# Merge stage of a transformer block: one written order on four engines, and two kinds of weight and activation splits on VectorE

## The chip, the cores and the metric

The kernel runs on one core of a Trainium2 chip. Its engines take instructions from queues of their own: PE (TensorE, matrix products), DVE (VectorE), ACT (ScalarE), POOL (GpSimd) and SP (SyncE, which here only issues DMA transfers). The metric is the device time of one execution in microseconds (us). It is the median over several runs.

## The reference

One layer over 2048 latent tokens of width 1024 with a context of 256 tokens. What matters here is the last part of the token-mixing half: two branch results are projected to the model width, gated, added, and projected once more onto the residual.

```python
def branch_merge(attn_o, gm_o, ga_logit, gb_logit, w_br_attn, w_br_gm, w_out):
    y = jax.nn.sigmoid(ga_logit) * (attn_o @ w_br_attn) + jax.nn.sigmoid(gb_logit) * (gm_o @ w_br_gm)
    return y @ w_out
...
        x = x + g1 * branch_merge(attn_x, gm_x, ga_x, gb_x, w_br_attn[l], w_br_gm[l], w_out[l])

        h2 = modulate(x, norm2_g[l], sh2, sc2)
        x = x + g2 * sq_relu_mlp(h2, w_ff1[l], w_ff2[l])
```

`attn_o` and `gm_o` are 2048 x 512, `w_br_attn` and `w_br_gm` 512 x 1024, `w_out` 1024 x 1024. Everything is float32.

## The kernel before

A float32 product is made of three products of rounded operands. Each operand is split in a high part (a cast on ACT, line 144 in `split`) and a low part (the operand less its high part, line 148, on POOL or DVE as the argument `lo_eng` says); `mm3` (lines 176 to 178) then multiplies high by high, high by low and low by high. Line 177 needs the low part of the moving operand, line 178 that of the stationary one.

The merge (`merge`) comes after attention and before the feed-forward half. It works through four blocks of 512 tokens (`NB`), each in two stages.

- **Branch stage.** Eight steps m (`KC`), one for each 128 output channels. A step has 24 matmuls: 12 for the gMLP branch "g" and 12 for the attention branch "a", into two of the eight PSUM banks. Then DVE multiplies each bank by its gate (line 910, twice), adds the two (line 913), and the sum y(m) is split: high on ACT, low on POOL.
- **Output product.** Four token tiles of 128 (tt), two halves n of 512 columns each: 192 matmuls of y with the split `wo` of `w_out`. The first tile runs k = 0 to 6 for both halves before k = 7, so that y(7) is needed last. After each half DVE scales (line 954) and adds to the residual tile `xt` (line 955); the tile is stored (line 957) and ACT sums its squares (line 960).

Three flows feed this. `fetch` is called at the start of step m and brings the branch weights (`br_raw`, line 859, tile `bw`, 14 slots), splits them (`br_weights`) and brings the gates (`gate_in`, line 874, tile `gt`, 6 slots) for the step two ahead, also over the border between blocks: at steps 6 and 7 it fetches for steps 0 and 1 of the next block, at step 0 for step 2. While the output product of block b runs, the generator `br_inputs(b + 1)`, moved on after each half, loads the next block's branch inputs (line 838; for attention also the softmax scales, line 842, multiplied in by DVE on line 848) and splits them into tile `in`. The slots of `raw` (3), `xt` (3) and `bw` make a load wait until whatever read the slot before is done. Block 0's branch stage also loads and splits `w_out` (line 826, tiles `ws` and `wo`).

The order of the instructions on an engine is set by a scheduler that weighs costs and slots; a written order holds only where `order()` adds a dependence. That function runs at the very end over all instructions: those in `pinned` ranges, and on PE and DVE those in `fixed` ranges, on SP those in `loads` ranges, are made to follow the one written before them on their engine. No such range lies in the merge's blocks, so there the scheduler chooses:

```python
            held = idx in pinned or (idx in fixed and i.engine in engines)
            held = held or (idx in loads and i.engine == self.nc.sync.engine)
            after = keys + ([i.engine] if held else [])
            for prev in {last[k].name for k in after if k in last}:
                self.tc.add_manual_dep(i, prev, dep, reason="order")
```

In this merge 20 of the 64 low splits of branch weights are on DVE (block 0's fetches and the first two), the other 44 and all 32 low splits of y on POOL. Low splits of `in` and `wo` are on DVE.

Of the kernel before, what the change touches and what calls it, by code (L numbers as in the profile page):

```python
# [67 lines left out]
class Kern:  # L68
    def __init__(self, ctx, tc, I, out):
        self.tc, self.nc, self.I, self.out = tc, tc.nc, I, out  # L70
        self.ctx = ctx
        self.uid = 0
        self.tags = {}
        self.pins = []
        self.fixed = []
        self.loads = []
        self.open_pools, self.pool_of = {}, {}
        self.banks = None
# [780 lines left out]
            self.nc.sync.dma_start(out[nm], src.rearrange("(k p) c -> p k c", p=P))  # L859
        return out  # L860

    def br_weights(self, raw, lo_eng="pool"):
        ws = {}
        for nm in ("g", "a"):
            wh, wl = self.sb("bw", [4, P], F32R), self.sb("bw", [4, P], F32R)
            self.split(raw[nm], wh, wl, lo_eng=lo_eng)
            ws[nm] = (wh, wl)
        return ws

# [8 lines left out]
    def merge(self, first, start, last):  # L878
        nc = self.nc
        for _ in start:  # L880
            pass
        self.close("mid", "base")
        self.open("out")
        self.open("branch")
        steps = [(b, m) for b in range(NB) for m in range(KC)]
        it = iter(steps)
        q = []
        w_out = self.load_w_out()

        def fetch(lo_eng="pool"):  # L890
            s = next(it, None)
            if s is not None:
                q.append((self.br_weights(self.br_raw(s[1]), lo_eng), self.gate_in(*s)))

        inp = first
        early = [(s, self.br_raw(s[1])) for s in (next(it), next(it))]
        for s, raw in early:
            q.append((self.br_weights(raw, "dve"), self.gate_in(*s)))
        for b in range(NB):
            y = []  # L900
            for m in range(KC):
                fetch("pool" if b else "dve")
                ws, gt = q.pop(0)
                for nm in ("g", "a"):
                    ps = self.bank([TB])
                    wh, wl = ws[nm]
                    for k in range(4):
                        h, l = inp[nm][k]
                        self.mm3(ps, wh[:, k, :], wl[:, k, :], h, l, k == 0, k == 3)
                    nc.vector.scalar_tensor_tensor(  # L910
                        out=gt[nm], in0=gt[nm], scalar=1.0, in1=ps, op0=ALU.add, op1=ALU.mult
                    )
                nc.vector.tensor_tensor(out=gt["a"], in0=gt["a"], in1=gt["g"], op=ALU.add)
                yh, yl = self.sb("y", [TB], F32R), self.sb("y", [TB], F32R)
                self.split(gt["a"], yh, yl)
                y.append((yh, yl))
                if b == 0:
                    next(w_out, None)
                    if m == 2:
                        last.sums(self.sb("raw", [TB]))  # L920
                    if m == 4:
                        last.inverse()
            inp = {}
            if b + 1 < NB:
                side = self.br_inputs(b + 1, inp)
            else:
                self.close("branch", "pre")
                self.open("early", side="right")
                side = self.h_early()
                next(side)  # L930
            for tt in range(TT):
                tok = slice(tt * P, (tt + 1) * P)
                xt = self.sb("xt", [D])
                nc.sync.dma_start(xt, self.x_block(b)[tok, :])
                banks = [self.bank([512]) for _ in range(2)]

                def outer(n, ks):
                    cs = slice(n * 512, (n + 1) * 512)
                    for k in ks:
                        self.mm3(  # L940
                            banks[n], y[k][0][:, tok], y[k][1][:, tok], self.wo[k][0][:, cs],
                            self.wo[k][1][:, cs], k == 0, k == KC - 1,
                        )

                head = KC - 1 if tt == 0 else KC
                if tt == 0:
                    for n in range(2):
                        outer(n, range(head))
                for n in range(2):
                    cs = slice(n * 512, (n + 1) * 512)  # L950
                    ps = banks[n]
                    outer(n, range(head if tt == 0 else 0, KC))
                    part = self.sb("jk", [512])
                    nc.vector.tensor_tensor(out=part, in0=ps, in1=self.g1b[:, cs], op=ALU.mult)
                    nc.vector.tensor_tensor(out=xt[:, cs], in0=xt[:, cs], in1=part, op=ALU.add)
                    next(side, None)
                nc.sync.dma_start(self.x1_d[b][tok, :], xt)
                junk = self.sb("jk", [D], mybir.dt.bfloat16)
                col = b * TT + tt
                nc.scalar.activation(  # L960
                    junk, xt, AF.Square, accum_out=self.ss2[:, col : col + 1]
                )
            for _ in side:
                pass
# [477 lines left out]
    def order(self):  # L1442
        dep = mybir.DependencyInfo(mybir.DependencyClass.NoSync, mybir.DependencyReason.DATA)
        last, seen = {}, set()
        pinned = {n for r in self.pins for n in r}
        fixed = {n for r in self.fixed for n in r}
        loads = {n for r in self.loads for n in r}
        engines = (self.nc.tensor.engine, self.nc.vector.engine)
        for idx, i in enumerate(list(self.nc.cur_bb.bb.instructions)):
            keys = []  # L1450
            for o in i.outs:
                n = getattr(getattr(o, "bass_ap", None), "name", None)
                if n in self.tags and n not in seen:
                    seen.add(n)
                    keys.append(self.tags[n])
            held = idx in pinned or (idx in fixed and i.engine in engines)
            held = held or (idx in loads and i.engine == self.nc.sync.engine)
            after = keys + ([i.engine] if held else [])
            for prev in {last[k].name for k in after if k in last}:
                self.tc.add_manual_dep(i, prev, dep, reason="order")  # L1460
            for k in keys + [i.engine]:
                last[k] = i
# [242 lines left out]
```

## Time and profile before

| | |
|---|---|
| median of 3 runs | 3104.24 us (3098.3 to 3105.01) |
| the profiled execution | 3103.83 us, of which the profile's span is 3102.0 us (1.83 us lie around it) |
| mean granted clock of TensorE | 0.994 |
| busy: PE, DVE, ACT, POOL | 3042.7, 1972.1, 1356.6, 704.1 us |
| matmuls | 13892 |
| the merge's blocks (branch stage of block 0 to the start of the feed-forward half) | 1456.2 to 1830.5 us from the span's start |

The profile is of one execution. A row of a group reads: line, engine, operation, out<-in with buffer numbers left out, shapes, count, then the sum of busy time and the mean ns of one, then the idle time of the engine just before them and what ended it. L148 and L144 are lines of the helper `split`, so the tile tells which use is meant: `bw`, `y`, `in` or `wo`. In the table by stage, each engine has its busy us and instruction count, and the last three numbers are the granted TensorE clock, the busy share of the DMA engines and GB/s. POOL, DVE and ACT work on 128 x 512 tiles here, and PE's matmul of a step is 128 x 128 by 128 x 512.

### The profile page before, as it was taken

The numbers are of one execution on the slowest core, as the hardware profiler recorded it, in microseconds if no ns is written. First come the engines' busy times: TensorE is split into PE (matmuls) and PEld (weight loads), VectorE is DVE, ScalarE is ACT, GpSimd is POOL, SyncE is SP. The second block draws the span as 40 slices with busy tenths as digits, with TensorE's granted clock in tenths as the row PEclk, the third lists the DMA queues.
The fourth block names the chain that finished last, engine by engine and source line by source line (L and its number), as shares of the span: only waits on it lengthen the run. The fifth ranks groups of instructions, "written<-read, shape, count | busy, mean of one in ns | idle before, by whom it ended". The sixth has DMA issues, their size and how long they took to land.

```text
span 3102.0 us, 37971 instructions
## 1 busy us (share of the span) xinstructions
PE 3042.7 (98%) x13892; PEld 2299.5 (74%) x13892; DVE 1972.1 (64%) x2893; ACT 1356.6 (44%) x2058; POOL 704.1 (23%) x539
## 2 busy tenths in 40 slices
PE   8999999999999999999999999999999999999999
PEld 4888888887555555555877878887777888888777
DVE  5837576576776767667643488876654676654545
ACT  4443435342555554544322255444543344444433
POOL 0000000010888888886144300000000000000000
PEclk9999999999999999999999999999999999999999
DMA  6354756544000000003754548887575644445565
GB/s 218 111 175 120 226 156 192 165 142 132 26 14 15 15 4 18 11 8 118 253 180 156 164 148 320 315 306 256 201 246 210 210 150 155 157 147 192 204 216 204
DMA packets 332173, 485.42 MB, mean 156 GB/s; under 512 B 33969, under 2 KB 166321, under 8 KB 331986
## 3 DMA queue, kind: packets, MB, share of 16 engines
q1 hardware_dynamic: 324002, 478.38, 46.3%
q10 hardware_dynamic: 7984, 4.61, 0.5%
q8 instruction: 109, 1.79, 0.2%
q14 instruction: 78, 0.64, 0.1%
HBM read 348.56 MB, written 134.35 MB: 156 GB/s over the span
## 4 chain that ended last, share of the span: by engine, by line
PE 89%; DMA 5%; DVE 3%; ACT 1%; issue 1%; POOL 1%; SPq 0%; DVEq 0%; ACTq 0%; POOLq 0%
PE b L1196 12%; PE b L1197 12%; PE b L1195 11%; PE b L176 10%; PE b L178 10%; PE b L177 10%; PE b L1597 8%; PE b L1564 5%; PE b L1583 4%; PE b L1529 3%; PE b L182 2%; DMA f<-w2o_d 1%; DMA bw<-in_w_br_gm 1%; POOL bw L148 1%; DMA f<-x_d 1%
## 5 line engine op out<-in xcount | busy, mean ns | idle before, releaser
L1292 DVE TENSOR_TENSOR f<-f,f 128x1024 fp32r<-128x1024 f32 x224 | 273.2, 1224 | 274.6 <-ACT f L1291 271.0
L1540 DVE TENSOR_REDUCE ts<-b 128x1 f32<-128x512 f32 x512 | 314.6, 681 | 173.2 <-PE b L1529 173.2
L1291 ACT CAST f<-f 128x1024 fp32r<-128x1024 f32 x224 | 235.2, 1053 | 335.3 <-DMA f<-ao_d 288.9
L1196 PE MATMUL b<-f,f 128*128 128x512 f32 x896 | 351.3, 392 | 4.6 <-DVE f L1292 4.0
L1197 PE MATMUL b<-f,f 128*128 128x512 f32 x896 | 349.6, 390 | 0.0
L1195 PE MATMUL b<-f,f 128*128 128x512 f32 x896 | 307.4, 392 | 10.3 <-ACT b L1334 4.7
L1613 POOL TENSOR_TENSOR ac<-ac,p 128x512 f32<-128x512 f32 x216 | 296.6, 1406 | 71.1 <-ACT p L1587 70.4
L1587 ACT ACTIVATE p<-b 128x512 f32<-128x512 f32 x384 | 199.4, 615 | 159.3 <-PE b L1583 142.5
L1613 POOL TENSOR_TENSOR ac<-ac,t 128x512 f32<-128x512 f32 x160 | 231.9, 1476 | 1.4 <-ACT t L1587 1.4
L1196 PE MATMUL b<-hl,f 128*128 128x512 f32 x576 | 224.9, 391 | 1.6 <-DVE hl L971 1.5
L1195 PE MATMUL b<-hl,f 128*128 128x512 f32 x576 | 224.1, 389 | 0.0
L1197 PE MATMUL b<-hl,f 128*128 128x512 f32 x576 | 224.0, 389 | 0.0
L148 DVE TENSOR_TENSOR w<-w,w 128x1024 fp32r<-128x1024 f32 x120 | 146.6, 1222 | 99.1 <-ACT w L144 70.6
L1195 PEld LDWEIGHTS b<-f,f 128*128 128x128 f32 x896 | 168.1, 188 | 51.0 <-ACT f L1291 6.8
L176 PE MATMUL b<-t,w 128*128 128x512 f32 x512 | 202.8, 396 | 0.1
L1196 PEld LDWEIGHTS b<-f,f 128*128 128x128 f32 x896 | 168.8, 188 | 45.7 <-DVE f L1292 11.2
L1564 PE MATMUL b<-t,t 128*128 128x512 f32 x576 | 198.4, 415 | 1.7 <-ACT p L1587 1.6
L178 PE MATMUL b<-t,w 128*128 128x512 f32 x512 | 199.7, 390 | 0.0
L177 PE MATMUL b<-t,w 128*128 128x512 f32 x512 | 199.5, 390 | 0.0
L1197 PEld LDWEIGHTS b<-f,f 128*128 128x128 f32 x896 | 168.5, 188 | 34.6
L176 PE MATMUL b<-w,t 128*128 128x512 f32 (+1 forms) x528 | 191.0, 362 | 1.0 <-ACT t L440 1.0
L144 ACT CAST w<-w 128x1024 fp32r<-128x1024 f32 x120 | 126.1, 1050 | 150.0 <-DMA w<-in_w_in 118.3
(226 smaller groups left out, 6289.6 us busy)
## 6 DMA issues: line engine op xcount, KB each, us to landing
w<-in_w_in SPq DMA_DIRECT2D x120, 512.0 KB
ao_d<-f SPq DMA_DIRECT2D x224, 256.0 KB
f<-ao_d SPq DMA_DIRECT2D x112, 512.0 KB
f<-w2o_d SPq DMA_DIRECT2D x112, 512.0 KB
f<-in_w_ff SPq DMA_DIRECT2D x48, 1024.0 KB
w2o_d<-f SPq DMA_DIRECT2D x112, 256.0 KB
md<-in_w_mod SPq DMA_DIRECT2D x32, 512.0 KB
f<-x_d SPq DMA_DIRECT2D x64, 256.0 KB
```

Of the source, the lines that this page charges most:

```text
L176: mm(ps, sh, mh, start=start, stop=False)
L177: mm(ps, sh, ml, start=False, stop=False)
L178: mm(ps, sl, mh, start=False, stop=stop)
L1195: mm(ps, wh, hh, start=start and k == 0, stop=False, skip_group_check=True)
L1196: mm(ps, wh, hl, start=False, stop=False, skip_group_check=True)
L1197: mm(ps, wl, hh, start=False, stop=k == len(w) - 1, skip_group_check=True)
L1291: nc.scalar.copy(h, f32(l))
L1292: nc.vector.tensor_tensor(out=l, in0=f32(l), in1=f32(h), op=ALU.subtract)
L1540: nc.vector.tensor_reduce(out=self.mx[:, t, h, c : c + 1], in_=ps[h], axis=AX.X, op=ALU.max)
L1564: self.nc.tensor.matmul(self.pts[j][h], k.KA[c][self.kv][:, ks], self.qa[h], start=True, stop=False, skip_group_check=True,)
L1597: nc.tensor.matmul(self.o[h * HD : (h + 1) * HD, :], k.V[c][:, i, self.kv * HD : (self.kv + 1) * HD], pt[h], start=j == 0, stop=j == NKT - 1,)
L1613: nc.gpsimd.tensor_tensor(out=self.acc[e][:, h], in0=old[:, h], in1=pt[h], op=ALU.add)
```

## The change

Every low split of the branch weights and of y is now made on DVE; POOL has nothing left in the merge (it loses 76 instructions, DVE gains 76). And a new range, from the end of block 0's branch stage to the end of block 3's branch stage, is held in written order on every engine but SP. SP stays with the scheduler, whose choice there comes out differently as well. On PE the order of all instructions is the same as before.

```diff
         self.fixed = []
+        self.steady = []
...
-    def br_weights(self, raw, lo_eng="pool"):
+    def br_weights(self, raw):
...
-            self.split(raw[nm], wh, wl, lo_eng=lo_eng)
+            self.split(raw[nm], wh, wl, lo_eng="dve")
...
-                self.split(gt["a"], yh, yl)
+                self.split(gt["a"], yh, yl, lo_eng="dve")
...
             inp = {}
+            if b == 0:
+                begin = self.here()
             if b + 1 < NB:
                 side = self.br_inputs(b + 1, inp)
             else:
+                self.steady.append(range(begin, self.here()))
                 self.close("branch", "pre")
...
+        steady = {n for r in self.steady for n in r}
...
             held = idx in pinned or (idx in fixed and i.engine in engines)
+            held = held or (idx in steady and i.engine != self.nc.sync.engine)
             held = held or (idx in loads and i.engine == self.nc.sync.engine)
```

The lines of the changed file lie one to six further down (L144 is L145, L148 is L149, L859 is L860, L874 is L875, L910 is L911, L960 is L964).

First place: ACT at the end of block 1's branch stage, before the change. y_14211 and y_14260 are the high parts of y(6) and y(7) of block 1; bw_14219, bw_14223, bw_14576 and bw_14580 are high parts of branch weights for block 2; in_ tiles are block 2's branch inputs.

```order
L144 CAST y_14162<-gt_14031 128x512
L144 CAST bw_14219<-bw_14217 128x512
L144 CAST bw_14223<-bw_14215 128x512
L144 CAST in_14318<-raw_14316 128x512
L144 CAST in_14330<-raw_14328 128x512
L144 CAST y_14211<-gt_14080 128x512
L144 CAST in_14370<-raw_14368 128x512
L144 CAST bw_14576<-bw_14574 128x512
L144 CAST bw_14580<-bw_14572 128x512
L144 CAST in_14403<-raw_14401 128x512
L144 CAST y_14260<-gt_14129 128x512
```

The same place after the change.

```order
L145 CAST y_14162<-gt_14031 128x512
L145 CAST bw_14170<-bw_14168 128x512
L145 CAST bw_14174<-bw_14166 128x512
L145 CAST y_14211<-gt_14080 128x512
L145 CAST bw_14219<-bw_14217 128x512
L145 CAST bw_14223<-bw_14215 128x512
L145 CAST y_14260<-gt_14129 128x512
L145 CAST in_14318<-raw_14316 128x512
L145 CAST in_14330<-raw_14328 128x512
L964 ACTIVATE jk_14335,ss_78<-xt_14264 128x1024
```

y(6) had four casts between itself and y(5), and y(7) four more; now each has the two weight casts of the fetch that is written ahead of it, and the casts of `in` and bw_14576 stand behind y(7).

Second place: DVE in a middle step of block 1's branch stage, before the change. gt_13933 and gt_13935 are the gates of step 3, gt_13982 and gt_13984 those of step 4.

```order
L910 SCALAR_TENSOR_TENSOR gt_13935<-gt_13935,b_14035 128x512
L910 SCALAR_TENSOR_TENSOR gt_13933<-gt_13933,b_14049 128x512
L913 TENSOR_TENSOR gt_13933<-gt_13933,gt_13935 128x512
L910 SCALAR_TENSOR_TENSOR gt_13984<-gt_13984,b_14084 128x512
L910 SCALAR_TENSOR_TENSOR gt_13982<-gt_13982,b_14098 128x512
```

The same steps after the change; bw_14073 and bw_14077 are low parts of the weights of step 6, bw_14122 and bw_14126 of step 7, and y_14114 is the low part of y(4); the gates here are those of step 4.

```order
L149 TENSOR_TENSOR bw_14073<-bw_14070,bw_14072 128x512
L149 TENSOR_TENSOR bw_14077<-bw_14068,bw_14076 128x512
L911 SCALAR_TENSOR_TENSOR gt_13984<-gt_13984,b_14084 128x512
L911 SCALAR_TENSOR_TENSOR gt_13982<-gt_13982,b_14098 128x512
L914 TENSOR_TENSOR gt_13982<-gt_13982,gt_13984 128x512
L149 TENSOR_TENSOR y_14114<-gt_13982,y_14113 128x512
L149 TENSOR_TENSOR bw_14122<-bw_14119,bw_14121 128x512
L149 TENSOR_TENSOR bw_14126<-bw_14117,bw_14125 128x512
```

A step had three instructions on DVE and now has six (of step 4 both low parts of weights, two gate products, the sum and the low part of y), and the two weight splits of a later step stand in front of the gate products.

Third place: SP's loads in the middle of block 1's branch stage, before the change; the weights are those of steps 5 and 6, gt_13982 and gt_13984 the gates of step 4, gt_14031 a gate of step 5.

```order
L859 DMA bw_14019<-in_w_br_attn 128x4x128
L874 DMA gt_13982<-ta_d_96 128x512
L859 DMA bw_14021<-in_w_br_gm 128x4x128
L874 DMA gt_13984<-tb_d_100 128x512
L859 DMA bw_14068<-in_w_br_attn 128x4x128
L874 DMA gt_14031<-ta_d_96 128x512
```

The same place after the change; the bw_ tiles are weights of steps 5 and 6, gt_14031 and gt_14033 the gates of step 5, which wait for tiles of step 2 to come free: gt_14031 for the sum on line 914, gt_14033 for the low split of y(2).

```order
L860 DMA bw_14019<-in_w_br_attn 128x4x128
L860 DMA bw_14021<-in_w_br_gm 128x4x128
L875 DMA gt_14031<-ta_d_96 128x512
L875 DMA gt_14033<-tb_d_100 128x512
L860 DMA bw_14068<-in_w_br_attn 128x4x128
L860 DMA bw_14070<-in_w_br_gm 128x4x128
```

Both weights of a step are now issued ahead of its gates, and the gates are those of a step one further on.

More of the change, by code (lines that the diff above doesn't have):

```diff
@@ L888, in merge, with fetch @@
         w_out = self.load_w_out()
-        def fetch(lo_eng="pool"):
+        def fetch():
             s = next(it, None)
             if s is not None:
-                q.append((self.br_weights(self.br_raw(s[1]), lo_eng), self.gate_in(*s)))
+                q.append((self.br_weights(self.br_raw(s[1])), self.gate_in(*s)))
         inp = first
@@ L897, in merge @@
         for s, raw in early:
-            q.append((self.br_weights(raw, "dve"), self.gate_in(*s)))
+            q.append((self.br_weights(raw), self.gate_in(*s)))
         for b in range(NB):
@@ L901, in merge @@
             for m in range(KC):
-                fetch("pool" if b else "dve")
+                fetch()
                 ws, gt = q.pop(0)
```

## The prediction

> **What bounds the kernel now.** I read the page's chain that ended last first, by engine, then the table by stage over the merge (branch stage, output product, in turn for blocks 0 to 2).
>
> ```profile
> PE 89%; DMA 5%; DVE 3%; ACT 1%; issue 1%; POOL 1%; SPq 0%; DVEq 0%; ACTq 0%; POOLq 0%
> ...
> 1456.20:1504.40 48.20, 47.89 (x197) 37.93 (x198) 35.00 (x47) 21.62 (x32) 10.01 (x7) 0.94 0.90 299
> 1504.40:1547.90 43.50, 43.50 (x193) 36.03 (x192) 22.97 (x32) 12.02 (x21) 4.38 (x3) 1.00 0.70 235
> 1547.90:1591.40 43.50, 43.50 (x193) 36.04 (x192) 17.05 (x23) 11.43 (x20) 22.17 (x17) 1.00 0.49 151
> 1591.40:1642.00 50.60, 47.25 (x194) 37.69 (x193) 22.47 (x29) 11.52 (x20) 9.22 (x8) 0.93 0.56 182
> 1642.00:1685.50 43.50, 43.50 (x194) 36.03 (x193) 16.24 (x23) 11.41 (x20) 22.52 (x17) 1.00 0.49 152
> 1685.50:1736.40 50.90, 46.10 (x194) 36.78 (x193) 21.71 (x29) 11.52 (x20) 9.56 (x8) 0.97 0.51 165
> ```
>
> PE sets the time: 192 matmuls of a stage take 43.50 us, 0.2266 us each and 5.44 a step, wherever nothing holds it. Two stages take longer with the same work: the output products of block 1 (50.60) and block 2 (50.90). What PE waited for between 1456 and 1830 us (us, times, longest):
>
> ```profile
> PE b L176 <- ACT y L144: 5.9, 2, 3.0
> ...
> PE b L178 <- POOL y L148: 2.1, 3, 1.1
> PE b L178 <- DVE bw L148: 0.3, 1, 0.3
> ```
>
> The 5.9 are one wait in each of the two slow stages, for the high part of y(6). The timeline of PE shows that such a wait costs more than its length:
>
> ```profile
> 1598.64 0.80 PE L176 MATMUL b<-wo,y 128*128 128x512 f32 x1 [2.97 <-ACT y L144]
> 1599.23 0.63 PE L177 MATMUL b<-wo,y 128*128 128x512 f32 x1
> ...
> 1607.77 0.39 PE L177 MATMUL b<-wo,y 128*128 128x512 f32 x1
> ```
>
> After 2.97 us without work matmuls last 0.63 to 0.80 us, later 0.39 again. That is why the stage's busy time is 47.25 instead of 43.50, at a granted clock of 0.93.
>
> Why y is late is in the chain of waits in order of time, at that place:
>
> ```profile
> 1598.40 2.53 DMA bw<-in_w_br_gm
> 1601.01 0.63 ACT bw L144
> 1601.77 1.29 POOL bw L148
> ...
> 1603.70 0.53 ACT in L144
> 1604.25 1.36 DVE in L148
> 1605.61 0.61 DVE gt L913
> 1606.24 0.63 ACT y L144
> 1606.94 1.30 POOL y L148
> 1608.28 0.50 PE b L178
> ```
>
> Nothing in y(7) needs branch weights or `in` of the next block. They stand ahead of it in the queues of ACT and DVE only because the scheduler put them there, and the weights wait for a load whose slot POOL's split sets free. Y pays for a loop DMA, ACT, POOL that belongs to another block.
>
> **The change part by part.** Durations of one, from the groups of instructions between 1456 and 1830 us:
>
> ```profile
> L910 DVE SCALAR_TENSOR_TENSOR gt<-gt,b 128x512 f32<-128x512 f32 x64 | 43.8, 685 | 77.2 <-PE b L178 77.1
> L913 DVE TENSOR_TENSOR gt<-gt,gt 128x512 f32<-128x512 f32 x32 | 24.3, 760 | 0.9
> L955 DVE TENSOR_TENSOR xt<-xt,jk 128x512 f32<-128x512 f32 x31 | 22.2, 724 | 0.7
> L148 DVE TENSOR_TENSOR bw<-bw,bw 128x512 fp32r<-128x512 f32 x20 | 13.8, 711 | 11.7 <-ACT bw L144 11.7
> L148 POOL TENSOR_TENSOR bw<-bw,bw 128x512 fp32r<-128x512 f32 x44 | 59.3, 1361 | 167.1 <-ACT bw L144 158.8 <-DMA gt<-ta_d 8.3
> L148 POOL TENSOR_TENSOR y<-gt,y 128x512 fp32r<-128x512 f32 x32 | 43.4, 1356 | 64.9 <-ACT y L144 64.9
> ```
>
> *Splits moved.* POOL loses 59.3 + 43.4 = 102.7 us, none of it on PE's path but where the waits above name it. DVE gains 76 x 0.711 = 54 us. A branch step on DVE is then 2 x 0.711 + 2 x 0.685 + 0.76 + 0.711 = 4.26 us, and about 0.7 more idle for the cast of y: 5.0 of PE's 5.44. It fits, by 0.4. Cost: nothing while DVE keeps step; if not, see the third rival.
>
> *Written order, y.* Counted from E, the end of a branch stage on PE: last gate product and sum of step 7 (0.685 + 0.76), cast (0.63 in the chain), low split (0.71) and hand-overs make y(7) ready by E + 3.5. The first tile runs 42 matmuls before it, 42 x 0.2266 = 9.5 us. y(6) is a step earlier, ready about E - 2, needed after 18 matmuls, at E + 4.1. Both waits vanish with their slow clock: 50.60 - 43.50 = 7.1 and 50.90 - 43.50 = 7.4, together **-14.5 us**.
>
> [...]
>
> *Next block's inputs, now behind the output.* What is late next is the last attention input, on which DVE's written order puts the product with the scales after the last sum of the output product, at T0 + 1.6 (T0: PE starts the next branch stage; scaling and sum of 0.7 each, with hand-overs). Product, cast and split (0.7 to 0.8 each) give the high part at T0 + 3.1, the low one at T0 + 3.9; PE wants the low one after 22 matmuls, T0 + 5.0. Cover: 1.1 us. Its scales can be issued once the third product has read its slot, T0 - 3.1, and how long such a load takes is seen on SP and DVE:
>
> ```profile
> 1601.83 1.09 SPq L842 DMA_DIRECT2D raw<-rs_d  x2
> 1606.97 1.80 DVE L848 TENSOR_TENSOR raw<-raw,raw 128x512 f32<-128x512 f32 x1 [0.76 <-DMA raw<-rs_d]
> 1708.05 1.09 SPq L842 DMA_DIRECT2D raw<-rs_d  x2
> 1712.13 0.69 DVE L848 TENSOR_TENSOR raw<-raw,raw 128x512 f32<-128x512 f32 x1 [0.28 <-DMA raw<-rs_d]
> ```
>
> 4.1 to 5.1 us: landing at T0 + 1.0 to T0 + 2.0, at worst 0.4 late of 1.1 us cover. I take 0. If every such load takes 5.1, load, product and issue (0.8) are a loop of 5.9 for each half tile of 5.44; three rounds add 1.4, 0.3 beyond the cover, at three borders +0.9.
>
> *Block 0's branch stage* is not held, but its eight y splits come to DVE: 35.00 + 8 x 0.711 = 40.7 of 48.20. SP's order there changes too: the loads of step 7's weights stand behind a gate load that waits for the sum of step 4. Before they stood ahead of it (weights, gate, cast):
>
> ```profile
> 1491.21 0.50 SPq L859 DMA_DIRECT2D bw<-in_w_br_gm  x1
> 1493.80 0.34 SPq L874 DMA_DIRECT2D gt<-ta_d  x1
> 1497.26 1.15 ACT L144 CAST bw<-bw 128x512 fp32r<-128x512 f32 x2 [0.25 <-DMA bw<-in_w_br_gm]
> ```
>
> The load took 6.0 us and was 0.3 late (the DVE wait above). Issued between 1491 and 1494 it is 0 to 3 us later. Without the wait the gain would be 0.6 (output product 1 lost 7.1 for 50.60 - 47.25 = 3.35 without work, so 0.3 is worth 0.6). I take +0.8, nearer to no delay, since on DVE step 4's sum now also stands ahead of the split of step 6's weights and of two `wo` splits. Bounds -0.6 and +3.
>
> *Block 3's end.* DVE makes y(7)'s low part, with its wait 1.4 us, before the feed-forward's first scaling; that has a cover:
>
> ```profile
> 1790.32 0.69 DVE L954 TENSOR_TENSOR jk<-b,g 128x512 f32<-128x512 f32 x1 [2.57 <-PE b L178]
> ```
>
> DVE idled 2.57 us ahead of this instruction, right behind that scaling, and the list of PE's waits has none for the scaling's result: 0, and up to +1.4 were that cover gone.
>
> Sum: -14.5 + 0.8 = -13.7 us. The profiled run's 3103.83 becomes 3090.1; it lies 0.4 under the median of the three, so against that **3090.5 us**. Bounds: -14.5 - 0.6 = -15.1 and, with all unknowns bad, -14.5 + 3 + 0.9 + 1.4 = -9.2.
>
> **Rivals.**
>
> *1. A new wait takes half of it.* The last attention input, or step 7 of block 0, holds PE for 2 to 3 us, and as at 1598.64 the clock drops with it, doubling the cost: -14.5 + 6 = 8 to 9 us gained, 3095. For: only 1.1 us of cover, and stores of 512 KB now stand ahead of the scales. Against: their loads' rows. [...]
>
> *2. The change doesn't do what it says.* SP is still free, so weights or gates come late enough that ACT, now bound to written order, keeps y behind a weight cast that waits for its load: y(7) still has two weight casts ahead of it. If each of the two stages loses what it loses now, 3104. For: the casts of the next block's step 1 do stand there. Against: their slots come free once PE has read the first half of step 6, at E - 8.2, and y(7)'s cast is due at E + 1.6; the longest such load in blocks 1 to 3 takes 5.3:
>
> ```profile
> 1569.60 0.38 SPq L859 DMA_DIRECT2D bw<-in_w_br_gm  x1
> 1574.94 1.14 ACT L144 CAST bw<-bw 128x512 fp32r<-128x512 f32 x2 [6.99 <-DMA bw<-in_w_br_gm]
> ```
>
> *3. Slower: a loop DVE, SP, DMA becomes the bound.* In written order the weight splits of step s+2 stand ahead of step s's gate products on DVE. If the load is late, these wait; the low part of y(s) follows; the gate load of step s+3 waits for that, and behind it on SP stands the next weight load. Around the loop: load time L, casts and two splits 2.1, two gate products, sum, cast and split of y 3.5, two issues 0.8, so L + 6.4 for two steps of 10.88. It decides at L = 4.5. The chain's load took 2.53, the row above 5.3. Block 0, with `w_out` loads beside, has 7.5:
>
> ```profile
> 1469.96 0.50 SPq L859 DMA_DIRECT2D bw<-in_w_br_gm  x1
> 1477.43 0.62 ACT L144 CAST bw<-bw 128x512 fp32r<-128x512 f32 x1 [0.52 <-DMA bw<-in_w_br_gm]
> ```
>
> With 7.5 throughout, each block slips 4 x 3.0 = 12 us, of which 3.7 are covered (issued 3.0 us into step s-1 and wanted 16.3 after that step's start, 16.3 - 3.0 - 7.5 - 2.1): 8.3 x 3 = 25, so -13.7 + 25 = +11, 3115. Against it: blocks 1 and 2 move 151 and 152 GB/s in their branch stages, block 0 299. [...]
>
> **How the numbers follow.** The forecast's case (3089 to 3095) 0.60; rival 1, 0.20; rival 2, with whatever leaves less than 6.2 us either way, 0.12; rival 3, 0.08. 6.2 us, 0.2%, is about the least that a measurement of this kernel can tell from no change. Faster is the first two, 0.80; same 0.12; slower 0.08. The range reaches up to rival 1's far end, 3099, and leaves out the other two; below, 3104.24 - 15.1 = 3089.1, and 2 more since the three runs themselves lie 6.7 apart: 3087.
>
> **What would show it.** Right: output products 1 and 2 at 43.5 us and clock 1.00, no PE wait on y, POOL idle, branch stages still 43.5 with DVE some 35 busy in each. Rival 1: a PE wait on `in` 4.8 us after an output product, or on `bw` near 1499. Rival 2: PE still waiting for y. Rival 3: branch stages over 43.5 and PE waiting for `bw` on DVE. Wrong altogether if the time goes to a stage outside the merge: the order there is the same.

## The result and the profile after

| | before | after |
|---|---|---|
| median, four runs each | 3101.27 us (3097.21 to 3105.01) | 3084.86 us (3080.37 to 3086.56) |
| ratio | | 0.9942 (95% interval 0.9930 to 0.9953) |
| profiled execution | 3103.83 us, span 3102.0 | 3084.55 us, span 3082.7 |

The medians lie 16.4 us apart, the profiled executions 19.3. The table by stage of the changed kernel, from block 0's branch stage to block 2's output product and on to the start of the feed-forward half:

```profile
1456.50:1503.65 47.15, 47.15 (x196) 37.86 (x197) 39.24 (x56) 22.97 (x34) 0.00 (x0) 0.95 0.96 312
1503.65:1547.17 43.52, 43.52 (x193) 36.04 (x192) 19.54 (x30) 8.53 (x15) 0.00 (x0) 1.00 0.58 196
1547.17:1590.69 43.52, 43.52 (x193) 36.04 (x192) 31.19 (x49) 14.85 (x26) 0.00 (x0) 1.00 0.70 207
1590.69:1634.21 43.52, 43.52 (x193) 36.04 (x192) 18.25 (x28) 7.91 (x14) 0.00 (x0) 1.00 0.50 155
1634.21:1677.73 43.52, 43.52 (x193) 36.04 (x192) 31.31 (x49) 14.85 (x26) 0.00 (x0) 1.00 0.70 212
1677.73:1721.25 43.52, 43.52 (x193) 36.04 (x192) 18.14 (x28) 7.91 (x14) 0.00 (x0) 1.00 0.47 151
1721.25:1764.77 43.52, 43.52 (x193) 36.04 (x192) 29.30 (x45) 12.72 (x22) 0.00 (x0) 1.00 0.48 145
```

Every stage from block 0's output product on takes 43.52 us at clock 1.00. What PE waited for between 1456 and 1815 us is one row, where the merge begins:

```profile
PE b L177 <- ACT bw L145: 5.4, 1, 5.4
```

The groups of instructions show DVE's work; the splits of weights and of y are all there, none takes more than 0.69 us on the mean:

```profile
L911 DVE SCALAR_TENSOR_TENSOR gt<-gt,b 128x512 f32<-128x512 f32 x64 | 42.1, 681 | 8.0 <-PE b L179 8.0
L149 DVE TENSOR_TENSOR bw<-bw,bw 128x512 fp32r<-128x512 f32 x64 | 41.8, 687 | 26.5 <-ACT bw L145 26.4
L149 DVE TENSOR_TENSOR y<-gt,y 128x512 fp32r<-128x512 f32 x32 | 22.1, 691 | 18.0 <-ACT y L145 18.0
L149 DVE TENSOR_TENSOR in<-raw,in 128x512 fp32r<-128x512 f32 x24 | 16.5, 688 | 8.9 <-ACT in L145 8.9
```

`in` fell from 945 to 688 ns. In the profile before, the 14 of its splits that no POOL instruction overlapped took 691 ns on the mean and the other ten 1300; after, POOL does nothing here. Over the whole span the difference of the two profiles divides as follows, by the start of PE's first matmul of each part; the feed-forward part is counted from its first matmul on the tile `hl` (the expectations of the first four experiments count it from 6.1 us earlier):

| part | before | after | difference |
|---|---|---|---|
| to the merge's first matmul | 1456.2 | 1456.5 | +0.3 |
| block 0, first 72 branch matmuls | 19.1 | 18.8 | -0.3 |
| block 0, other 120 | 28.08 | 27.34 | -0.7 |
| output product of block 1 | 50.54 | 43.52 | -7.0 |
| output product of block 2 | 50.91 | 43.52 | -7.4 |
| feed-forward part, to the end | 1265.4 | 1261.3 | -4.1 |

The last row has the same instructions in the same order. Most of it lies in one stretch, in which PE waited 10.1 us before and 9.0 after, and the granted clock differs (before, then after):

```profile
2098.80:2313.50 214.70, 204.28 (x902) 165.44 (x901) 137.21 (x167) 108.03 (x141) 0.00 (x0) 0.98 0.68 236
```

```profile
2083.50:2292.91 209.41, 200.25 (x901) 162.72 (x900) 136.56 (x167) 107.84 (x141) 0.00 (x0) 1.00 0.71 242
```

### The profile page after: what moved, and what is told of

It is laid out like the page before. It is cut to its first block, busy times and chain, and to the rows that moved or that the text cites. A ratio compares the mean times of both kernels' runs of the same rounds, so it can differ in the third digit from the quotient of the medians.

```text
span 3082.7 us, 37890 instructions
## 1 busy us (share of the span) xinstructions
PE 3032.2 (98%) x13892; PEld 2294.3 (74%) x13892; DVE 2005.0 (65%) x2969; ACT 1355.5 (44%) x2058; POOL 601.7 (20%) x463
## 4 chain that ended last, share of the span: by engine, by line
PE 91%; DVE 4%; DMA 3%; ACT 1%; issue 1%; SPq 0%; DVEq 0%; ACTq 0%
PE b L1200 12%; PE b L1201 12%; PE b L1199 11%; PE b L177 11%; PE b L179 11%; PE b L178 11%; PE b L1603 8%; PE b L1570 5%; PE b L1589 4%; PE b L1535 3%; PE b L183 2%; DVE f L1296 1%; DMA f<-w2o_d 1%; DMA f<-ao_d 1%; DMA ts<-in_b_mod 1%
## 5 line engine op out<-in xcount | busy, mean ns | idle before, releaser
L149 DVE TENSOR_TENSOR w<-w,w 128x1024 fp32r<-128x1024 f32 x120 | 146.6, 1222 | 100.1 <-ACT w L145 71.6
L145 ACT CAST w<-w 128x1024 fp32r<-128x1024 f32 x120 | 126.1, 1051 | 151.4 <-DMA w<-in_w_in 120.7
```

## The experiments

Each is compared with the kernel before on the same chip. In the first four that had a median of 3102.73 us, in the next four 3101.43; beside the two with more instructions on DVE it ran once, 3100.58. Where an experiment has one run, its stages tell more than its total: two runs of the kernel before on one chip lie up to 10 us apart (3099.65 and 3109.79).

The theory of the prediction was that y's place in ACT's queue costs the time, so that the written order brings the gain. The rival: GpSimd's slow splits (1.36 us each before, 0.71 on DVE).

**Splits alone** (`e1_splits_only`): the change without its written order.

```diff
             held = idx in pinned or (idx in fixed and i.engine in engines)
-            held = held or (idx in steady and i.engine != self.nc.sync.engine)
```

> The low splits of branch weights and y on VectorE as in the change, but no written order; the scheduler again puts casts of the next block's weights and inputs ahead of y(6) and y(7) on ScalarE. Theory (the place of y in ScalarE's queue is what costs): the stalls in the output products of blocks 1 and 2 stay, shorter by the 0.6 us that each of some four low splits ahead of y(6) saves, so 1 to 5 us lost in each instead of 7.0 and 7.4; total gain on before 5 to 12 us. Rival (GpSimd's slow splits, 1.36 us against 0.7, are the cause): both output products at 43.5 us, gain 14 to 15 us. For the feed-forward part (from its first matmul to the end, 1271.5 us before and 1267.3 us in the change's profile, with the same instructions in the same order): if the 4 us are chance, anything from 1265 to 1273; if they come with the earlier start of that part, between the two in proportion to the gain.

Measured: 3086.43 us, ratio 0.9943 (0.9930 to 0.9957). Both output products take 43.52 us. The theory falls: the scheduler's order on ACT is as before, y(6) behind two casts of weights and two of inputs, and nothing is lost. ACT's timeline at the end of block 1's branch stage before, where PE ends at 1591.4:

```profile
1594.35 0.62 ACT L144 CAST bw<-bw 128x512 fp32r<-128x512 f32 x1 [3.61 <-DMA bw<-in_w_br_gm]
1596.41 0.62 ACT L144 CAST bw<-bw 128x512 fp32r<-128x512 f32 x1 [1.44 <-POOL bw L148]
1596.93 1.13 ACT L144 CAST in<-raw 128x512 fp32r<-128x512 f32 x2
1597.97 0.61 ACT L144 CAST y<-gt 128x512 fp32r<-128x512 f32 x1
```

And with the splits on DVE, where it ends at 1590.8:

```profile
1585.08 1.14 ACT L145 CAST bw<-bw 128x512 fp32r<-128x512 f32 x2 [1.60 <-DMA bw<-in_w_br_gm]
1586.12 1.22 ACT L145 CAST in<-raw 128x512 fp32r<-128x512 f32 x2
1588.26 0.62 ACT L145 CAST y<-gt 128x512 fp32r<-128x512 f32 x1 [0.92 <-DVE gt L914]
```

The same sequence, but against the stage's end the weights have landed 8.7 us earlier; y(6) waits for its own sum alone and is cast 2.6 us before that end instead of 6.5 us behind it.

**Order alone** (`e2_order_only`): the written order as in the change, the splits on GpSimd as before.

```diff
-            self.split(raw[nm], wh, wl, lo_eng="dve")
+            self.split(raw[nm], wh, wl, lo_eng=lo_eng)
...
-                self.split(gt["a"], yh, yl, lo_eng="dve")
+                self.split(gt["a"], yh, yl)
```

> The written order on four engines as in the change, the low splits left on GpSimd as before. Theory: y is cast behind two weight casts only, so both output products take 43.5 us; gain in the merge 14 us, block 0 as before (0.9 over its matmuls in the second half). Rival (GpSimd's slow splits are the cause): y(6) and y(7) still wait for them, 3 us or more lost in each of the two output products, gain under 9 us. Feed-forward part: 1265 to 1273 us if chance, about 1267 if it follows the earlier start.

Measured: 3087.71 us, ratio 0.9945 (0.9930 to 0.9959). Both output products take 43.52 us, as the theory had it; block 0's 120 matmuls took 29.46, longer than before (28.08). So each half of the change does the whole by itself, which neither theory had said.

**Order on one engine.** ScalarE alone, with the splits on GpSimd (`e3_act_order_only`), and VectorE alone, with the splits of the change (`e4_dve_order_only`).

```diff
-            held = held or (idx in steady and i.engine != self.nc.sync.engine)
+            held = held or (idx in steady and i.engine == self.nc.scalar.engine)
```

```diff
-            held = held or (idx in steady and i.engine != self.nc.sync.engine)
+            held = held or (idx in steady and i.engine == self.nc.vector.engine)
```

> Written order on ScalarE alone, everything else left to the scheduler, low splits on GpSimd as before. Theory: y's place on ScalarE is enough for y(6)'s high part; on VectorE and GpSimd the scheduler may still put splits ahead of y(7)'s sum and low part, so the output products of blocks 1 and 2 lose 0 to 2 us each. Rival (the order on VectorE matters as much): 3 us or more in each. Feed-forward part: 1265 to 1273 us if chance.

> Low splits on VectorE as in the change, written order on VectorE alone; ScalarE is left to the scheduler, whose choice comes out near the written one all the same, with one cast of the next block's inputs ahead of y(6). Theory: 0 to 1 us lost in each of the output products of blocks 1 and 2; at the borders between blocks one weight cast stands behind the last input cast, so 0 to 1 us there. Rival (ScalarE has to be held): 3 us or more in each. Feed-forward part: 1265 to 1273 us if chance.

Measured: 3088.57 and 3085.58 us, one run each; 43.52 us in all four output products. That ScalarE suffices agrees with the theory, but after the first run it separates nothing: whatever was touched, the stall went. What is needed is something that all of these runs change.

They share the loading of the weights. SP's issues of one of the two weight loads of each step in block 1's branch stage, before:

```profile
1555.71 0.39 SPq L859 DMA_DIRECT2D bw<-in_w_br_gm  x1
...
1591.62 0.38 SPq L859 DMA_DIRECT2D bw<-in_w_br_gm  x1
1598.40 0.38 SPq L859 DMA_DIRECT2D bw<-in_w_br_gm  x1
```

And after:

```profile
1552.89 0.49 SPq L860 DMA_DIRECT2D bw<-in_w_br_gm  x1
...
1584.54 0.46 SPq L860 DMA_DIRECT2D bw<-in_w_br_gm  x1
1590.04 0.46 SPq L860 DMA_DIRECT2D bw<-in_w_br_gm  x1
```

Before, seven issues in 42.69 us: 7.1 each, while PE takes 5.44 a step. After, eight in 37.15: 5.3. The slots say why. Before, a weight load waits for the slot that POOL's low split of the step just before frees; after, it waits for PE's matmuls of the third step back. What SP waited for between 1548 and 1600 us shows it, before:

```profile
SPq L859 <- POOL bw L148: 19.7, 10, 4.6
```

And after:

```profile
SPq L860 <- PE b L178: 1.5, 4, 0.4
SPq L860 <- PE b L179: 0.4, 1, 0.4
```

In `e2_order_only`, with the splits on GpSimd, the weight loads there wait for PE as well, and none for POOL. The chain of waits that the prediction quotes is the loop: load, ACT, POOL, ACT, POOL, load. It is slower than PE, so the weights fall behind by 1.7 us a step, 10 us over these six, and y, on ACT behind them, with them. The new theory is this load loop.

**Which split** (`e5_y_on_dve`, `e6_bw_on_dve`): the kernel before with one of the two moved.

```diff
-                self.split(gt["a"], yh, yl)
+                self.split(gt["a"], yh, yl, lo_eng="dve")
```

```diff
-                fetch("pool" if b else "dve")
+                fetch("dve")
```

> The kernel before with the low splits of y alone on VectorE; branch weights stay on GpSimd, no written order. New theory (the weight loads of blocks 1 to 3 form a loop: a load waits for the slot that GpSimd's split of the step before frees, some 7 us a step in the profile before against PE's 5.44, the weights fall behind and y stands behind them on ScalarE): the loop stays, both output products lose 5 to 8 us, no gain beyond 3 us. Rival (GpSimd's time for y itself makes y late): both lose under 2 us.

> The kernel before with the low splits of the branch weights alone on VectorE; y stays on GpSimd, no written order, and y still stands behind the next block's weights on ScalarE. New theory (the load loop): the loop is shorter and its slots come free otherwise, weights are issued every 5.4 us in the branch stages and both output products lose under 1 us. Rival (GpSimd's time for y): both lose 3 us or more.

Measured: y on DVE 3097.86 us, output products 50.78 and 51.87; weights on DVE 3086.32 us, both 43.52. As the load loop has it, though the issues with the weights on DVE are 5.8 us apart (seven from 1555.30 to 1589.92) and not the 5.4 expected. PE's waits with y on DVE, between 1460 and 1830 us, are of the same kind as before:

```profile
PE b L176 <- ACT y L144: 7.6, 2, 3.9
PE b L178 <- DVE y L148: 0.9, 2, 0.6
```

The issues there are still seven in 43.4 us (1551.12 to 1594.53), 7.2 each. Moving y's splits is worth nothing for the stalls: they cost 7.3 and 8.4 us. The time of this one run lies 3.6 us under the median of the kernel before, where at most 3 was expected, and 1.5 under the lowest of its seven (3099.35); block 0, which takes 27.34 us for its 120 matmuls, gives 0.7 of it.

**Slots of their own** (`e9_raw_own_slots`): neither part of the change; the same 14 slots, divided.

```diff
-    "branch": {"gt": 6, "bw": 14, "ws": 2},
+    "branch": {"gt": 6, "br": 6, "bw": 8, "ws": 2},
...
-            out[nm] = self.sb("bw", [4, P])
+            out[nm] = self.sb("br", [4, P])
```

> The kernel before, with the 14 weight slots divided: 6 for the loaded weights and 8 for their two parts, so that a load waits for the split three steps back instead of one. Every split stays on its engine, no written order, y stays behind casts of the next block on ScalarE. New theory (the load loop): weights are issued every 5.4 us, both output products lose under 1 us, 14 us gained without either part of the change. Rival (y's place on ScalarE, or GpSimd's 1.36 us, costs by itself): both lose 3 us or more.

Measured: 3085.90 us, ratio 0.9953 (0.9936 to 0.9969); no wait of PE at all in the merge's blocks between 1460 and 1815 us, both output products 43.52. GpSimd still makes 76 splits, which took 1.36 us each in the profile before, and four casts of the next block's weights and inputs still stand between y(5) and y(6) on ACT, and four more before y(7). The loads keep PE's step exactly:

```profile
1552.64 0.38 SPq L859 DMA_DIRECT2D br<-in_w_br_gm  x1
1558.08 0.38 SPq L859 DMA_DIRECT2D br<-in_w_br_gm  x1
1563.52 0.38 SPq L859 DMA_DIRECT2D br<-in_w_br_gm  x1
```

**The loop put back** (`e12_order_serial_load`): the written order, splits on GpSimd, two slots for the loads.

```diff
-    "branch": {"gt": 6, "bw": 14, "ws": 2},
+    "branch": {"gt": 6, "br": 2, "bw": 12, "ws": 2},
```

> Written order on four engines with the low splits on GpSimd, and the loop put back: of the 14 weight slots 2 are for the loaded weights and 12 for their parts, so that a load waits for the split of the step before. New theory (the load loop): at 7 us a step against 5.44 the weights fall behind, and since y no longer stands behind them PE waits in the branch stages themselves, 3 to 8 us in each of blocks 1 to 3: 9 to 24 us slower than the written order alone, 3097 to 3112. Rival (the written order cures the stall whatever the loads do): branch stages of 43.5 us, 3085 to 3090.

Measured: 3099.58 us, one run. The issues in block 1 are 6.7 us apart, the stages of blocks 1 to 3 take 44.91, 44.39, 45.45, 44.43 and 44.53: 6.1 us over 5 x 43.52, less than the 9 to 24 expected; block 0, in which the two slots hold as well, has 36.02 for the 120 matmuls instead of 29.46, as much again. So the total lies in the expected range only because block 0 paid too, which the expectation had not counted. PE's waits in blocks 1 to 3 (the first rows between 1510 and 1835 us):

```profile
PE b L179 <- POOL bw L149: 2.4, 5, 0.6
PE b L179 <- POOL y L149: 1.0, 2, 0.5
```

PE now waits mostly for the weights themselves, not for a y behind them: the output products of blocks 1 and 2 lose 0.9 us each. With a slow loop in place the written order leaves 6.1 us lost where the scheduler's loses 14.4, for it frees y, but it does not cure the loop. That it cured all in the other runs goes with loads that waited for PE and not for POOL.

**Room on VectorE** (`e8_two_more_dve`, `e8_four_more_dve`): the change with 2 or 4 more instructions on DVE in each step.

```diff
                 y.append((yh, yl))
+                for _ in range(2 if b else 0):
+                    nc.vector.tensor_tensor(out=self.spare, in0=gt["a"], in1=gt["a"], op=ALU.add)
```

> The change with two more VectorE instructions (a sum of a gate tile with itself into a tile nobody reads, 128x512) behind y in each branch step of blocks 1 to 3. VectorE was busy 31.2 of 43.5 us in these stages, 3.9 a step, and waits some 0.7 for the cast of y; with 2 x 0.62 a step takes 5.85 against PE's 5.44. If the loop of VectorE, SP and DMA has the lead of about 7.7 us that the prediction's third rival works out with the loads as they are, a lag of 8 x 0.4 = 3.3 is covered: all stages at 43.5, the time of the change. If VectorE's 0.4 us of spare time was all the cover there is: 1 to 3 us lost in each of three blocks.

> The same with four more VectorE instructions a step: 3.9 + 0.7 + 4 x 0.62 = 7.1 us a step against 5.44, a lag of 13 us over eight steps. With a lead of 7.7: 5 to 7 us lost in each of blocks 1 to 3, in the last branch steps or at y, 15 to 20 us in all, more with the slow clock behind. If the lead is larger than 13: nothing lost.

Measured: 3092.89 and 3113.67 us. With two more, all stages of blocks 1 to 3 stay at 43.52, as expected with a lead; but 2.3 us are waited for at the start of the feed-forward's transposes. This is not only a late DVE: behind block 3's branch stage the scheduler chooses, and it chose otherwise here. The feed-forward's first scaling now stands behind a scaling of the output product, for which DVE idled 2.08 us:

```profile
1776.91 0.69 DVE L961 TENSOR_TENSOR jk<-b,g 128x512 f32<-128x512 f32 x1 [2.08 <-PE b L179]
1777.52 2.28 DVE L999 TENSOR_TENSOR f<-f,fs 128x2048 f32<-128x2048 f32 x1
```

In the change it stands ahead of it (1771.21, the output's at 1775.18). So this run does not measure the cover at block 3's end that the prediction put at 2.57 less 1.4. With four more, the issues are 7.4 us apart, the branch stages take 47.4, 46.9 and 46.9, the output products 47.0, and the end loses most:

```profile
PE b L183 <- DVE f L999: 9.4, 1, 9.4
PE b L179 <- DVE bw L149: 8.4, 6, 1.5
PE b L177 <- ACT y L145: 5.2, 5, 1.3
```

That is 7 us lost in each of blocks 1 and 2 and 3 in block 3's branch stage, where it was expected, and 9.4 in one piece at a place that was not, where the scaling again stands behind the output's scalings: from the merge's first matmul to the feed-forward's it is 396.1 us against 365.0, 31 more.

**Before, once more** (`e7_before_again`), for the 4 us in the feed-forward part.

> The kernel before once more, unchanged, for a second profile. From the first matmul of the feed-forward part to the end it took 1265.4 us in the first profile, 1260.3 to 1263.8 in those of the change and of every experiment, with and without the stalls. If the 4 us that the change's profile gains outside the merge are chance of one execution, this one takes 1260 to 1264 too, and the output products of blocks 1 and 2 again lose 13 to 16 us together. If they belong to the kernel before: 1265 or more.

Measured: 3099.49 us; a second run of the same kernel beside it took 3109.07. The feed-forward part took 1263.2 us, the output products 51.31 and 51.21, block 0's 120 matmuls 28.71. In all, the feed-forward part of the thirteen profiles lies between 1260.3 and 1265.4 us; the first one of before is the slowest, the next 1263.8. The run with y on DVE, whose stalls are those of before, has 1262.9. Chance of one execution, at least for the most part. The granted clock has a share in it: in the stretch shown above the first profile of before has two pieces of 3.41 us at half clock (from 2157.96 and 2198.92), the change's has none. It is not all: by estimate two such pieces cost 2 x 3.41 x 0.5 = 3.4 us, and the stretch is 5.3 us longer before. The merge by itself gives 15.4 us against the first profile of before (364.96 us from its first matmul to the feed-forward's, after 380.38) and 16.8 against the second (381.78), and the medians 16.4.

## Why the prediction was wrong, point by point

The range, 3087 to 3099, missed 3084.86 by 2.1 us. The direction and the size of the large term held; the step that failed is the term for block 0's branch stage. Of the 5.6 us between 3090.5 and 3084.86, 3.0 are the time the sum was made against, 1.5 block 0, 0.2 the rest of the merge, and 1.0 lie outside the merge, where no part of the change acts and the profiles vary. Against the range's lower end block 0 counts only 0.1, since that end had -0.6 for it; there the miss is 1.0 of base beyond the 2 allowed, and the variation outside the merge, for which the range had nothing.

- **Both stalls go, -14.5.** Measured -7.0 and -7.4, 14.4. y(6) was cast 2.9 us before PE ended the branch stage and y(7) at E + 1.65, where the prediction had y(7)'s cast at E + 1.6:

```profile
1587.75 0.62 ACT L145 CAST y<-gt 128x512 fp32r<-128x512 f32 x1 [2.76 <-DVE gt L914]
1588.38 1.14 ACT L145 CAST bw<-bw 128x512 fp32r<-128x512 f32 x2
1592.34 0.62 ACT L145 CAST y<-gt 128x512 fp32r<-128x512 f32 x1 [2.81 <-DVE gt L914]
```

- **Why they go.** The prediction saw the loop DMA, ACT, POOL and the slot that POOL frees, but credited the written order alone; that its -14.5 came true all the same is luck in part. Either part is enough, and so is a division of the slots. The loop, at 7.1 us a step, was the cause: without it nothing was lost with y in its old place. Y's place set the price: with the loop put back and y free, 6.1 us were lost instead of 14.4. No run moved y alone and left the loop exactly as it was.
- **Block 0, +0.8: the step that failed.** It had the sign wrong: -0.7 against the first profile of before, -1.4 against the second. The load of step 7's weights was said to come up to 3 us later, behind a gate load that waits for step 4's sum. The timeline of SP and ACT after shows the gate at 1490.13 and the load at the same time as before (1491.21), landed sooner:

```profile
1490.13 0.32 SPq L875 DMA_DIRECT2D gt<-ta_d  x1
...
1490.98 0.50 SPq L860 DMA_DIRECT2D bw<-in_w_br_gm  x1
```

  and its cast on ACT:

```profile
1495.58 1.14 ACT L145 CAST bw<-bw 128x512 fp32r<-128x512 f32 x2 [2.61 <-DMA bw<-in_w_br_gm]
```

  The sum of step 4, moved ahead on DVE, starts at 1489.49 instead of 1493.09, so the gate did not hold the load up. From issue to cast the load took 4.6 us instead of 6.0; why it was shorter is not shown. PE waited for nothing in these 120 matmuls (27.34 us, and 120 x 0.2266 is 27.2), so +0.8 was wrong by 1.5. The two profiles of before differ by 0.6 in this stage, so the size of the gain is uncertain, the sign of the term is not.
- **What the sum was made against.** The first three runs of before had a median of 3104.24; with the fourth it is 3101.27. The prediction's -13.7 from there is 3087.6. The range's lower end took two us for this, and three were needed. Its upper end, 3099, is worked out nowhere, and no run shows a term that leads there: rival 1's own sum gives 3095, and after the change PE waited neither for `in` nor, past the merge's start, for `bw`.
- **The last attention input** cost nothing. DVE waited for its scales twice, 0.6 us in all, and PE not at all.
- **DVE's room.** The change's branch stages of blocks 1 to 3 have DVE busy for 31.2, 31.3 and 29.3 us, where some 35 were forecast; there was more room than the 0.4 us a step of the prediction.
- **The clock.** What came back is 14.4 us and not the 8.2 of the time without work alone, (50.60 - 47.25) + (50.90 - 46.10): the slow matmuls behind the waits went too. In the profile before, waits of 2.97 and 2.92 us had matmuls of 0.63 to 0.80 us behind them, at granted clocks of 0.93 and 0.97 over the two stages. The last section shows what the record of the clock has there.
- **The third rival** did not come about with the loads as they are (5.3 us a step). Its price has no direct test: four more DVE instructions bring the loads to 7.4 us a step by another way and cost 7 us in each of blocks 1 and 2, where the prediction worked out 8.3 at 6.9 a step with loads of 7.5 us. What the end of block 3 adds, at the feed-forward, was overlooked.

## What to carry to other kernels

Where a wait ends in a queue behind another block's work, compare that work's issue period with the bound engine's step before blaming the order: here it was 7.1 against 5.44 us, and a pool in which a load takes the slot of the step just before makes such a loop. Giving loads and their products slots of their own (same memory, one line) was worth as much here as moving 76 instructions to another engine and writing the order by hand (3085.90 and 3084.86 us). And an instruction added to an engine with room in every stage can also be paid where the stages end and the order is free again, as the 2.3 and 9.4 us at the feed-forward's start show.

## What the runs showed of the hardware

A wait of PE was not followed by half clock every time, and its length alone does not tell what follows. After 2.92 us the first two matmuls took 0.50 and 0.40 us, and the slow ones began 1.5 us later:

```profile
1692.65 0.50 PE L176 MATMUL b<-wo,y 128*128 128x512 f32 x1 [2.92 <-ACT y L144]
1692.98 0.40 PE L177 MATMUL b<-wo,y 128*128 128x512 f32 x1
1694.12 0.79 PE L178 MATMUL b<-wo,y 128*128 128x512 f32 x1 [0.73 <-POOL y L148]
1694.71 0.63 PE L176 MATMUL b<-wo,y 128*128 128x512 f32 x1
```

With y on DVE, 3.70 us were followed at once by slow matmuls (0.80 and 0.63 us, for 6 us); with four more DVE instructions, waits of 1.09 and 1.27 us by none (0.50 and 0.40 us).

The profile before has the granted clock of the merge at one half in three pieces: from 1454.82 to 1461.64 us, from 1598.18 to 1605.01 and from 1693.75 to 1697.16, which is 6.83, 6.83 and 3.41 us. From the end of one to the next are 136.54 and 88.74 us, to the rounding 40 and 26 times 3.413. Three windows of 3.41 us around the wait above (after the length comes PE's busy time; the granted clock is third from the end):

```profile
1690.34:1693.75 3.41, 0.73 (x2) 0.30 (x2) 2.16 (x2) 2.70 (x5) 2.39 (x3) 1.00 0.03 10
1693.75:1697.16 3.41, 3.04 (x7) 2.47 (x8) 2.66 (x4) 0.74 (x2) 1.60 (x2) 0.50 1.00 329
1697.16:1700.58 3.42, 3.42 (x16) 2.64 (x15) 1.97 (x2) 1.38 (x3) 1.30 (x1) 1.00 0.70 198
```

PE idled 2.68 us of the first, and the second ran at half clock, though PE was busy for 3.04 us of it. Ahead of the pieces at 1454.82 and 1598.18 it idled 3.41 and 2.51 us of such a window. Of the others that these steps of 3.41 us give at full clock between 1461.64 and 1830.5 us, none has over 1.15 us idle and none has half clock behind it. After the change PE was busy all the time from 1461.36 to 1815.36 us, at clock 1.00. So in this merge the idle time within one window went with the clock. That it decides is the author's estimate: outside the merge half clock also follows, in the profile before, on windows with 1.88, 1.84, 1.63 and 0.20 us idle (from 2154.55, 2195.51, 1424.10 and 778.98), and full clock on one with 1.67 (2246.71). No run varied the phase by itself.
